# A two-layer hybrid encoder trunk on one core: own slots for two turned tiles, gates in two steps, memory rows later, last two quads by token tile

## Chip, cores and metric

The kernel runs on 1 core of one Trainium2 chip. The metric is device microseconds of one execution; the time given for a kernel is the median of its runs. Before the change it is 2223.97 us (3 runs, 2223.84 to 2224.96).

## What is computed

Input x (256 tokens x 2048 features, float32), a memory of 256 rows of the same width, and the weights of two layers. Each layer:

```
h    = rms_norm(x, norm_mix)
proj = h @ w_in          # g_q g_k 512 each, g_v g_r 1024 each, two gate ranks of 16, d_q d_k d_v m_q 512 each
mix  = concat( GLA(g_q, g_k, g_v, g_r, gates forward and backward),     # 4 heads, chunked, decays by log-sigmoid gates
               dilated window attention(d_q, d_k, d_v, relative bias),  # 4 heads
               attention of m_q to rms_norm(mem) @ w_mem_kv )           # 4 heads
x    = x + mix @ w_out
x    = x + square(relu(rms_norm(x) @ w_up)) @ w_down                    # 8192 wide
```

and one rms_norm at the end. All in float32.

## The kernel before

**Products.** Every large product goes through `linear` (L192): 256 tokens are two token tiles `t` of 128, the columns come 512 at a time into one PSUM bank per token tile, and the contraction in quads of 4 x 128 rows. A quad's weights (1 MB) are loaded by SP into one of three `raw` buffers (`load_quad`), ScalarE casts them to float32r (`wh`, L203), VectorE subtracts to get the low part (`wl`, L204), and TensorE makes three matmuls for each of 8 (row block, token tile) pairs: low x high, high x low, high x high (L221 to L223). `wh` and `wl` hold two quads. In the last quad of a product the matmuls are sorted by token tile.

**Left operands.** A left operand must lie transposed and split in the same way. x^T and mem^T of the first layer come transposed from the host (`split_loaded`). Everything else is turned on VectorE in 32x32 blocks, 16 instructions for a tile (`turn_blocks`, L108), then split (`parts_of`). `split_turned` and `heads_turned` are generators: `paced` makes the number of blocks that `steps` names and yields, and `turn(1)` advances the foremost one by a step. One `turn(1)` and one `flush(1)` (of `pending`, a queue of small jobs: squares of rows, loads) are called in each quad, behind that quad's last subtraction on VectorE. `turning` is first in, first out.

**Who sets the order.** The framework's planner orders the instructions of each engine by the order in which they are traced, by a timeline that it simulates, and by free buffers. A tile that finds no free slot waits, and what writes it is put later. Most tiles of 4 KB a partition share one ring of 22 slots (`slot`): turned and split operands, attention weights, gate tiles, `u` of the MLP. `work` has small pools: `junk` (2 buffers, target of squares whose sum alone is wanted), `E` (2 buffers of 6 KB), `dg` (2). `issue_after(i)` holds instructions of i's engine behind i.

**Start.** SP loads mem^T and the first three weight quads of the memory keys in turns, then `rel`, `onehot`, the memory rows (L497, four loads into x's buffer, for the sums of squares) and `ident`. The rest of the memory keys, the memory values (`ps_v`, in the auxiliary PSUM pool), column 9 of w_in (memory queries) and column 0 follow. When a chunk of memory rows has been squared, POOL loads the same chunk of x over it (L539). x^T is loaded by `plan_loads`, one step for each quad of the memory values.

**Mixing stage.** Column 1 (keys of GLA), memory attention (`attend_weights`, `attend_out`), `log_gates` (low-rank products, then exponential, logarithm, and a split into `gh`, `gl`), columns 2 and 3 (values of GLA), `gla_weights` (cumulative gates by matmuls with `tri`, exponentials into `E`, products with the turned queries and keys gqT and gkT), column 6 (dilated queries), and so on; then w_out, and the MLP in four parts of four groups of w_up and four of w_down.

**End.** After the last product each token tile adds its last chunk to x, sums squares, makes the reciprocal root on POOL (`rstd`) and scales four chunks on VectorE and ScalarE; SP stores them in two halves (L661 to L677).

Of the kernel before, what the change touches and what calls it, by code (L numbers as in the profile page):

```python
# [20 lines left out]
P = 128  # L21
# [21 lines left out]
def trunk_kernel(ctx: ExitStack, tc: tile.TileContext, a: dict):  # L43
# [12 lines left out]

    def turned_slot(name):
        return ring.tile([P, 4, S], F32, tag="o", name=name, bufs=2)
# [25 lines left out]
    class RowNorm:  # L84
# [6 lines left out]
        def add(self, c, t, v):  # L91
            junk = work.tile([P, NW], F32, tag="junk", name="junk")
            nc.scalar.activation(junk, v, AF.Square, accum_out=self.ssc[:, t, c:c + 1])  # L93
# [18 lines left out]
    def paced(turns, steps):  # L112
        for n in steps:
            for _ in range(n):
                next(turns)
            yield
# [75 lines left out]
    def linear(wsrc, lhs, quads, loaded=(), pool=ps_mm, tag="mm"):  # L192

        ps = [pool.tile([P, NW], F32, tag=tag, name=f"mm{t}") for t in range(NT)]
        nq = len(quads)
        for i, q in enumerate(quads):
            raw, n = loaded[i] if i < len(loaded) else load_quad(wsrc, q)
            wh = [wpool.tile([P, 2, NW], F32R, tag="wh", name="wh", bufs=4) for _ in range(2)]
            wl = [wpool.tile([P, 2, NW], F32R, tag="wl", name="wl", bufs=4) for _ in range(2)]
            n = min(4 // n, 2)  # L200
            for k in range(0, 4, n):
                hi, lo = (w[k // 2][:, k % 2:k % 2 + n] for w in (wh, wl))
                nc.scalar.activation(hi, raw[:, k:k + n], AF.Copy)  # L203
# [8 lines left out]
            xh, xl = lhs[q]  # L212
# [3 lines left out]
            for kk, t in order:  # L216
                sl = slice(t * P, (t + 1) * P)
                first = i == 0 and kk == 0
                last = i == nq - 1 and kk == 3
                hi, lo = wh[kk // 2][:, kk % 2, :], wl[kk // 2][:, kk % 2, :]  # L220
                nc.tensor.matmul(ps[t], xl[:, kk, sl], hi, start=first, stop=False)  # L221
                nc.tensor.matmul(ps[t], xh[:, kk, sl], lo, start=False, stop=False)  # L222
                nc.tensor.matmul(ps[t], xh[:, kk, sl], hi, start=False, stop=last)  # L223
            with tc.issue_after(cut.ins):
                flush(1)
        return ps
# [19 lines left out]
    tri = const.tile([P, 4, 2 * P], F32R, name="tri")  # L246
# [4 lines left out]
    onehot = work.tile([P, NW], F32, tag="junk", name="onehot")[:BUCKETS + 1]  # L251
# [12 lines left out]
    def late_constants():  # L264
        tri32 = work.tile([P, 4, 2 * P], F32, tag="E", name="tri32")
# [47 lines left out]
    def attend_out(weights, v, name):  # L313
# [5 lines left out]
        for t in range(NT):  # L319
            ps = aux([H, P], "pv")  # L320
            for h in range(H):
                for s in range(NT):
                    nc.tensor.matmul(  # L323
                        ps[:, h, :], pT[s][:, h, t * P:(t + 1) * P],
                        v[:, s, h * P:(h + 1) * P], start=s == 0, stop=s == NT - 1,
                    )
            ss = small.tile([P, H], F32, tag="ssh", name="ssh")
            for h in range(H):
                junk = work.tile([P, NW], F32, tag="junk", name="junk")
# [12 lines left out]

    def log_gates(lhs, rs, l):

        raw = slot([KT, 2 * RANK], "lrw")
# [5 lines left out]
        up32 = slot([2, NW], "up32")[:4 * RANK]  # L351
# [5 lines left out]
        gbias = slot([2, NW], "gbias")  # L357
# [12 lines left out]
        for d in range(2):  # L370
# [24 lines left out]
    def gla_weights(qT, kT, gates):  # L395
# [3 lines left out]
        for d in range(2):  # L399
            cr = slot([2, H, P], f"cr{d}")  # L400
            for i in range(NT):

                E = work.tile([P, 3, H, P], F32, tag="E", name="E")
                for h in range(H):
                    ps = aux([2 * P], "cum")
                    lo = slice(h * P, (h + 1) * P)
                    rhs = tri[:, 2 * d + i, :]
                    nc.tensor.matmul(ps, gl[d][:, i, lo], rhs, start=True, stop=False)
                    nc.tensor.matmul(ps, gh[d][:, i, lo], rhs, start=False, stop=True)
                    nc.scalar.activation(  # L410
                        E[:, 1:, h, :], ps.rearrange("p (b c) -> p b c", b=2), AF.Exp
                    )
                    nc.scalar.activation(E[:, 0, h, :], ps[:, :P], AF.Exp, scale=-1.0)
                tok = slice(i * P, (i + 1) * P)
                nc.vector.tensor_tensor(E[:, 0], kT[:, :, tok], E[:, 0], ALU.mult)
                nc.vector.tensor_tensor(E[:, 1], qT[:, :, tok], E[:, 1], ALU.mult)
# [3 lines left out]
                    cr[:, 0 if isk else 1], (kT if isk else qT)[:, :, tok], E[:, 2], ALU.mult  # L420
                )
                ps = aux([H, P], "dg")
                for h in range(H):
                    nc.tensor.matmul(ps[:, h, :], E[:, 0, h, :], E[:, 1, h, :], start=True, stop=True)  # L424

                dst = AT[i][:, i] if d == 0 else work.tile([P, H, P], F32, tag="dg", name="dg")
# [14 lines left out]
    def gla_out(AT, v):  # L441
        out = [slot([NT, NW], f"gla{c}") for c in range(2)]
        for c in range(2):
            for t in range(NT):
# [8 lines left out]
                for j in range(2):  # L453
                    junk = work.tile([P, NW], F32, tag="junk", name="junk")
# [45 lines left out]
    def plan_loads(name, loads, src, gain, lhs):  # L500


        def step(i):
            for q in loads[i] if i < len(loads) else ():
# [11 lines left out]
    for l in range(DEPTH):  # L516
# [4 lines left out]
        def keys_turned():  # L521
            turning.append(split_turned(km, "km", None, f"kmT{l}", heads, (0, 4, 4, 4, 4)))
# [6 lines left out]
        if l == 0:  # L529
            flush()  # L530
            bias_products()
            plan_loads("x0", ((0, 1), (2,), (3,)), a["xT"], gains[:, 0, 0, :], xlhs)
# [45 lines left out]
        mgain = gains[:, 1, l, :]  # L578
        turning.append(split_turned(o_mem, 3, mgain, "mT3", mlhs, (0, 4, 4, 4, 4)))
        gv = [evac(col(2 + c), rs, f"gv{c}") for c in range(2)]  # L580
# [39 lines left out]
        for part in range(FP):  # L620
            ulhs = {}
            for g in range(up_groups):
# [3 lines left out]
                u = slot([NT, NW], "u")  # L626
# [16 lines left out]
            for g in range(4):  # L643
# [4 lines left out]
                ps = linear(a["w_down"][l, part, g], ulhs, range(up_groups))  # L648
# [12 lines left out]
    for t in range(NT):  # L661
        v = xchunk(3, t)
        fnorm.add(3, t, v)
        rs = fnorm.done(t)
        for half in (1, 0):
            for c in (2 * half, 2 * half + 1):
                v = xchunk(c, t)
                if c == 3:
                    nc.vector.scalar_tensor_tensor(
                        v, v, rs[:, 0:1], fg[1][:, 1, :], ALU.mult, ALU.mult  # L670
                    )
                elif c == 1:
                    nc.vector.tensor_scalar(v, v, rs[:, 0:1], None, ALU.mult)
                else:
                    nc.scalar.activation(v, v, AF.Copy, scale=rs[:, 0:1])
            cs = slice(2 * half * NW, (2 * half + 2) * NW)
            nc.sync.dma_start(out_rows[:, t, cs], x[:, t, cs])  # L677
# [14 lines left out]
def _constants():  # L692
# [6 lines left out]
    for d, (inc, exc) in enumerate(((le, gt), (ge, lt))):  # L699
# [4 lines left out]
        for i in range(NT):  # L704
            isk = (i == 0) == (d == 0)
            sets.append(np.concatenate([middle, exc if isk else inc], 1))
# [70 lines left out]
```

## Time and profile before

| what | value |
|---|---|
| median of 3 runs | 2223.97 us |
| profiled execution | 2225.28 us, its span 2223.5 us |
| mean granted clock of TensorE | 0.994 |
| TensorE / VectorE / ScalarE busy | 98% / 71% / 51% |
| moved by DMA | 423.13 MB, mean 190 GB/s over the span |

The span runs from the first to the last instruction; the rest of an execution's time lies around it. In the rows PE is TensorE's matmuls, PEld its weight loads, DVE VectorE, ACT ScalarE, POOL GpSimd, SP the engine that issues most loads (SPq: the issuing instruction). A granted clock of 1.00 is 2.4 GHz, 0.50 is 1.2 GHz. A matmul's duration in the trace overlaps the next one's; the spacing of starts is what it takes.

### The profile page before, as it was taken

To read this page: it belongs to the slowest core of one execution; us is meant where nothing else is said; L and a number is where in the kernel's file an instruction comes from. 1 tells how busy PE (TensorE), PEld (TensorE's weight loads), DVE (VectorE), ACT (ScalarE), POOL (GpSimd) and SP (SyncE) were. 2 spreads that over 40 slices of the span, in tenths; PEclk is the share of its full clock that TensorE was granted. 3 is DMA by queue.
4 is the path that set the end of the run, shared out by engine and by line. 5 is a ranking of instruction groups with operands and counts; after the bars stand their busy time and mean duration, and the time that the engine had idled before them with its cause. 6 is when DMAs were issued, how large, how long until landed. Compare 5 with 4: busy or idle time off the path is not lost.

```text
span 2223.5 us, 25583 instructions
## 1 busy us (share of the span) xinstructions
PE 2184.5 (98%) x9834; PEld 1811.1 (81%) x9834; DVE 1588.5 (71%) x2210; ACT 1131.2 (51%) x1497; POOL 40.1 (2%) x69
## 2 busy tenths in 40 slices
PE   7998999999999999999999999999999999999998
PEld 5886888888888888888888887888888888888886
DVE  5658788886477577468977588788755764864774
ACT  7555565554354455345554554655544544543543
POOL 1000000000000000000000000000000000000000
PEclk9999999999999999999999999999999999999999
DMA  9643345555555555556555443455555555555553
GB/s 361 224 171 133 133 171 189 197 191 199 189 192 199 196 189 192 194 191 218 210 190 199 160 163 125 168 193 190 205 189 189 201 197 189 190 193 200 193 209 133
DMA packets 63362, 423.13 MB, mean 190 GB/s; under 512 B 7075, under 2 KB 7843, under 8 KB 14472
## 3 DMA queue, kind: packets, MB, share of 16 engines
q1 hardware_dynamic: 62104, 417.56, 53.8%
q0 software_dynamic: 1136, 3.94, 0.5%
q8 instruction: 77, 1.26, 0.2%
q14 instruction: 45, 0.37, 0.1%
HBM read 419.37 MB, written 3.15 MB: 190 GB/s over the span
## 4 chain that ended last, share of the span: by engine, by line
PE 94%; DVE 2%; DMA 2%; ACT 1%; issue 1%; SPq 0%; POOL 0%; ACTq 0%; POOLq 0%; DVEq 0%
PE mm L222 30%; PE mm L223 30%; PE mm L221 30%; DMA raw<-in_w_mem 1%; PE pv L323 1%; PE go L448 1%; DVE gkT L108 1%; DVE wl L204 0%; PE dg L424 0%; PE pT L309 0%; DVE gqT L108 0%; DMA x<-in_mem 0%; DVE dkT0o L108 0%; ACT junk L93 0%; ACT wh L203 0%
## 5 line engine op out<-in xcount | busy, mean ns | idle before, releaser
L204 DVE TENSOR_TENSOR wl<-raw,wh 128x1024 fp32r<-128x1024 f32 (+1 forms) x774 | 928.4, 1215 | 533.8 <-ACT wh L203 529.3
L203 ACT ACTIVATE wh<-raw 128x1024 fp32r<-128x1024 f32 (+1 forms) x774 | 813.9, 1053 | 887.2 <-PE mm L223 823.9
L222 PE MATMUL mm<-wl,uT2h 128*128 128x512 f32 x256 | 99.6, 389 | 0.0
L222 PE MATMUL mm<-wl,uT3h 128*128 128x512 f32 x256 | 99.6, 389 | 0.0
L223 PE MATMUL mm<-wh,uT3h 128*128 128x512 f32 x256 | 99.6, 389 | 0.0
L223 PE MATMUL mm<-wh,uT2h 128*128 128x512 f32 x256 | 99.6, 389 | 0.0
L221 PE MATMUL mm<-wh,zT0l 128*128 128x512 f32 x256 | 99.6, 389 | 0.0
L222 PE MATMUL mm<-wl,zT0h 128*128 128x512 f32 x256 | 99.6, 389 | 0.0
L223 PE MATMUL mm<-wh,zT0h 128*128 128x512 f32 x256 | 99.6, 389 | 0.0
L222 PE MATMUL mm<-wl,zT1h 128*128 128x512 f32 x256 | 99.6, 389 | 0.0
L223 PE MATMUL mm<-wh,zT1h 128*128 128x512 f32 x256 | 99.6, 389 | 0.0
L222 PE MATMUL mm<-wl,zT2h 128*128 128x512 f32 x256 | 99.6, 389 | 0.0
L223 PE MATMUL mm<-wh,zT2h 128*128 128x512 f32 x256 | 99.6, 389 | 0.0
L222 PE MATMUL mm<-wl,zT3h 128*128 128x512 f32 x256 | 99.6, 389 | 0.0
L223 PE MATMUL mm<-wh,zT3h 128*128 128x512 f32 x256 | 99.6, 389 | 0.0
L222 PE MATMUL mm<-wl,uT0h 128*128 128x512 f32 x256 | 99.6, 389 | 0.0
L223 PE MATMUL mm<-wh,uT0h 128*128 128x512 f32 x256 | 99.6, 389 | 0.0
L222 PE MATMUL mm<-wl,uT1h 128*128 128x512 f32 x256 | 99.6, 389 | 0.0
L223 PE MATMUL mm<-wh,uT1h 128*128 128x512 f32 x256 | 99.6, 389 | 0.0
L221 PE MATMUL mm<-wh,zT1l 128*128 128x512 f32 x256 | 99.4, 389 | 0.0
L221 PE MATMUL mm<-wh,uT1l 128*128 128x512 f32 x256 | 99.4, 389 | 0.0
L221 PE MATMUL mm<-wh,uT3l 128*128 128x512 f32 x256 | 99.3, 389 | 0.0
(428 smaller groups left out, 4637.5 us busy)
## 6 DMA issues: line engine op xcount, KB each, us to landing
raw<-in_w_up SPq DMA_DIRECT2D x128, 1024.0 KB, 4.8
raw<-in_w_down SPq DMA_DIRECT2D x128, 1024.0 KB, 4.8
raw<-in_w_in SPq DMA_DIRECT2D x80, 1024.0 KB, 4.8
raw<-in_w_out SPq DMA_DIRECT2D x32, 1024.0 KB, 4.8
raw<-in_w_mem SPq DMA_DIRECT2D x13, 1024.0 KB, 4.9
mem<-in_memT SPq DMA_DIRECT2D x7, 512.0 KB, 6.6
raw<-in_w_mem SPq DMA_DIRECT2D x12, 256.0 KB, 6.0
x<-in_mem SPq DMA_DIRECT2D x4, 512.0 KB, 6.8
```

Of the source, the lines that this page charges most:

```text
L108: yield nc.vector.transpose(dst[f:f + 32, :, :, s:s + 32], src[s:s + 32, :, :, f:f + 32])
L203: nc.scalar.activation(hi, raw[:, k:k + n], AF.Copy)
L204: cut = nc.vector.tensor_tensor(lo, raw[:, k:k + n], hi.bitcast(F32), ALU.subtract)
L221: nc.tensor.matmul(ps[t], xl[:, kk, sl], hi, start=first, stop=False)
L222: nc.tensor.matmul(ps[t], xh[:, kk, sl], lo, start=False, stop=False)
L223: nc.tensor.matmul(ps[t], xh[:, kk, sl], hi, start=False, stop=last)
L323: nc.tensor.matmul(ps[:, h, :], pT[s][:, h, t * P:(t + 1) * P], v[:, s, h * P:(h + 1) * P], start=s == 0, stop=s == NT - 1,)
L448: nc.tensor.matmul(ps[:, j, :], AT[s][:, t, 2 * c + j, :], v[c][:, s, j * DV:(j + 1) * DV], start=s == 0, stop=s == NT - 1,)
```

## The change

1. A second tag of two 4 KB slots in the ring's pool (`side_slot`) holds gqT, gkT and, in the MLP, `u`. `junk` and `dg` have one buffer each; `tri` holds three blocks of 128 columns for each direction in place of two pairs; the loads of `log_gates` go to `E` buffers.
2. `log_gates` ends with z and its clipped copy; exponential, logarithm and split are a function of their own, `gate_parts`, called after column 2's evacuation.
3. In layer 0 gk is evacuated before memory attention and both gq and gk are turned 8 blocks a step; in layer 1 memory attention stands before column 1. `paced` does not yield after its last step. Steps of km change.
4. What `turn` and `flush` issue on ScalarE in a quad is also held behind that quad's last cast.
5. The memory rows are loaded by the first four steps of x^T's plan, a chunk a step.
6. In the very last product the last two quads are ordered by token tile together, and the tail takes the sum of the first three chunks' squares ahead, skips one reduction, and stores in three pieces on two queues.

```diff
+    def side_slot(shape, name):
+        return ring.tile([P] + shape, F32, tag="t", name=name, bufs=2)
...
     def paced(turns, steps):
-        for n in steps:
+        for i, n in enumerate(steps):
             for _ in range(n):
                 next(turns)
-            yield
+            if i + 1 < len(steps):
+                yield
...
-    def heads_turned(v, name, heads):
+    def heads_turned(v, name, heads, steps):
-        o = slot([H, S], name)
-        yield from paced(turn_blocks(o, v), (0, 4, 4, 4, 4))
+        o = side_slot([H, S], name)
+        yield from paced(turn_blocks(o, v), steps)
...
-            with tc.issue_after(cut.ins):
+            with tc.issue_after(cut.ins), tc.issue_after(cast.ins):
                 turn(1)
...
-            order = [(kk, t) for kk in range(4) for t in range(NT)]
+            order += [(i, q, wh, wl, kk, t) for kk in range(4) for t in range(NT)]
+            if nq - late <= i < nq - 1:
+                continue
             if i == nq - 1:
-                order.sort(key=lambda o: o[1])
+                order.sort(key=lambda o: o[5])
...
+                    if late > 1 and t and done[0] is not None:
+                        queued.enter_context(tc.issue_after(done[0].ins))
...
-    tri = const.tile([P, 4, 2 * P], F32R, name="tri")
+    tri = const.tile([P, 2, 3 * P], F32R, name="tri")
...
-        raw = slot([KT, 2 * RANK], "lrw")
+        loaded = work.tile([P, 3, NW], F32, tag="E", name="lrup")
+        raw = loaded[:, 0].rearrange("p (k r) -> p k r", k=KT)
...
             nc.vector.scalar_tensor_tensor(ab[d], z[d], -1.0, z[d], ALU.mult, ALU.min)
+        return z, ab
+
+    def gate_parts(z, ab):
         for d in range(2):
             done = nc.scalar.activation(ab[d], ab[d], AF.Exp)
...
     with tc.issue_after(newest[0]):
-        for c in range(4):
+        nc.sync.dma_start(ident, a["ident"])
+
+    def load_rows(c):
+        with tc.issue_after(newest[0]):
             nc.sync.dma_start(x[:, :, c * NW:(c + 1) * NW], tokens(a["mem"], c))
-        nc.sync.dma_start(ident, a["ident"])
...
         def step(i):
+            if also is not None and i < 4:
+                also(i)
...
-            turning.append(split_turned(km, "km", None, f"kmT{l}", heads, (0, 4, 4, 4, 4)))
+            turning.append(split_turned(km, "km", None, f"kmT{l}", heads, (0, 6, 5, 5)))
...
-        turning.append(heads_turned(gq, "gqT", heads))
-        ps_gk = col(1)
-        while "mq" not in heads:
-            turn(1)
-        o_mem = attend_out(attend_weights(heads["mq"], heads["km"], None, "mem"), vm, "memo")
-        gk = evac(ps_gk, rs, "gk")
-        gates = log_gates(xlhs, rs, l)
-        turning.append(heads_turned(gk, "gkT", heads))
+        turning.append(heads_turned(gq, "gqT", heads, (0, 8, 8) if l == 0 else (0, 4, 4, 4, 4)))
+        if l == 0:
+            gk = evac(col(1), rs, "gk")
+            turning.append(heads_turned(gk, "gkT", heads, (0, 8, 8)))
+            o_mem = memory_attention()
+            gates = log_gates(xlhs, rs, l)
+        else:
+            o_mem = memory_attention()
+            gk = evac(col(1), rs, "gk")
+            gates = log_gates(xlhs, rs, l)
+            turning.append(heads_turned(gk, "gkT", heads, (0, 4, 4, 4, 4)))
         turning.append(split_turned(o_mem, 3, mgain, "mT3", mlhs, (0, 4, 4, 4, 4)))
-        gv = [evac(col(2 + c), rs, f"gv{c}") for c in range(2)]
+        gv = [evac(col(2), rs, "gv0")]
+        gates = gate_parts(*gates)
+        gv.append(evac(col(3), rs, "gv1"))
...
+                ending = end and last and g == 3
+                ps = linear(a["w_down"][l, part, g], ulhs, range(up_groups), late=2 if ending else 1)
+                if ending:
+                    continue
...
+        part = small.tile([P, 1], F32, tag="part", name="part")
+        nc.vector.tensor_reduce(part, fnorm.ssc[:, t, :3], AX.X, ALU.add)
+        nc.gpsimd.tensor_scalar(part, part, 1.0 / D, EPS, ALU.mult, ALU.add)
+        nc.vector.tensor_tensor(v, ps[t], v, ALU.add)
         fnorm.add(3, t, v)
-        rs = fnorm.done(t)
...
+        nc.gpsimd.tensor_scalar(m, fnorm.ssc[:, t, 3:], 1.0 / D, part[:, 0:1], ALU.mult, ALU.add)
...
+        nc.gpsimd.tensor_tensor(rs, m, neghalf[:, :1], ALU.pow)
...
+        nc.sync.dma_start(out_rows[:, t, :2 * NW], v[:, :2 * NW])
...
+        nc.sync.dma_start(out_rows[:, t, 3 * NW:], v[:, 3 * NW:])
...
+        nc.scalar.dma_start(out_rows[:, t, 2 * NW:3 * NW], v[:, 2 * NW:3 * NW])
```

## Rows read from the trace of the kernel before

**Rows 1.** The page, part 1: engine, busy us (share of the span), instructions.
```profile
PE 2184.5 (98%) x9834; PEld 1811.1 (81%) x9834; DVE 1588.5 (71%) x2210; ACT 1131.2 (51%) x1497; POOL 40.1 (2%) x69
```

**Rows 2.** Waits of TensorE: who waited <- for whom: us in total, times, longest.
```profile
PE mm L222 <- DVE wl L204: 18.4, 7, 9.9
PE mm L221 <- ACT wh L203: 10.4, 4, 5.1
```

**Rows 3.** Windows: length, busy us per engine, granted clock, DMA share, GB/s.
```profile
26.70:64.30 37.60, 30.32 (x122) 23.36 (x122) 20.82 (x31) 25.18 (x49) 5.59 (x10) 0.95 0.96 369
190.00:207.00 17.00, 7.14 (x25) 5.47 (x24) 16.56 (x33) 4.67 (x12) 0.00 (x0) 0.70 0.20 73
280.00:290.00 10.00, 8.50 (x38) 6.71 (x37) 9.90 (x15) 6.52 (x9) 0.00 (x0) 1.00 0.58 206
290.00:1290.00 1000.00, 1000.00 (x4504) 830.31 (x4502) 726.42 (x1008) 512.51 (x639) 11.65 (x14) 1.00 0.55 192
1290.00:1300.00 10.00, 7.94 (x28) 6.04 (x27) 9.83 (x16) 4.23 (x11) 0.00 (x0) 0.83 0.54 206
1370.00:1385.00 15.00, 12.04 (x48) 9.56 (x47) 14.75 (x26) 7.83 (x9) 0.00 (x0) 0.89 0.44 157
```

**Rows 4.** Timeline of TensorE, 200 to 207 us: start, us, what, [idle before <-releaser].
```profile
202.51 0.79 PE L222 MATMUL mm<-wl,x00h 128*128 128x512 f32 x1 [9.86 <-DVE wl L204]
...
205.66 0.39 PE L221 MATMUL mm<-wh,x00l 128*128 128x512 f32 x1
```

**Rows 5.** Timeline of TensorE, its last matmul.
```profile
2213.61 0.39 PE L223 MATMUL mm<-wh,uT3h 128*128 128x512 f32 x1
```

**Rows 6.** Timeline of VectorE, 186 to 205 us.
```profile
186.22 7.17 DVE L108 STREAM_TRANSPOSE gqT<-gq 32x256 f32<-32x256 f32 x16
193.42 7.18 DVE L108 STREAM_TRANSPOSE gkT<-gk 32x256 f32<-32x256 f32 x16
...
201.24 3.49 DVE L204 TENSOR_TENSOR wl<-raw,wh 128x1024 fp32r<-128x1024 f32 x3
```

**Rows 7.** The tile gqT: ns min/median/max, first and last start.
```profile
L108 DVE STREAM_TRANSPOSE gqT<-gq x32: 425/436/442, 186.2 to 1226.9; 32x256 f32<-32x256 f32 x32
```

**Rows 8.** Timeline of VectorE in layer 1, 1285 to 1376 us.
```profile
1285.09 7.18 DVE L108 STREAM_TRANSPOSE gkT<-gk 32x256 f32<-32x256 f32 x16
...
1370.77 2.69 DVE L108 STREAM_TRANSPOSE dkT1o<-dk 32x256 f32<-32x256 f32 x6
```

**Rows 9.** Timeline of TensorE, 1366 to 1384 us.
```profile
1376.38 0.79 PE L222 MATMUL mm<-wl,xT0h 128*128 128x512 f32 x1 [2.96 <-DVE wl L204]
```

**Rows 10.** Timeline of VectorE in an MLP group, 455 to 464 us.
```profile
457.63 2.36 DVE L204 TENSOR_TENSOR wl<-raw,wh 128x1024 fp32r<-128x1024 f32 x2
459.91 1.29 DVE L122 TENSOR_TENSOR uT0l<-uT0o,uT0h 128x512 fp32r<-128x512 f32 x2
```

**Rows 11.** Timeline of TensorE in the same group.
```profile
461.32 0.61 PE L221 MATMUL mm<-wh,zT3l 128*128 128x512 f32 x2
```

**Rows 12.** Timeline of SP (DMA issues), 13 to 36 us.
```profile
15.18 2.39 SPq L497 DMA_DIRECT2D x<-in_mem  x4
...
19.55 0.82 SPq L189 DMA_DIRECT2D raw<-in_w_mem  x2
```

**Rows 13.** DMA from 10 to 60 us; issues: xcount, KB each, us to landing.
```profile
DMA packets 5532, 19.27 MB, mean 385 GB/s; under 512 B 650, under 2 KB 778, under 8 KB 4575
...
raw<-in_w_mem SPq DMA_DIRECT2D x5, 1024.0 KB, 15.2
```

**Rows 14.** Timeline of TensorE, 26 to 31 us.
```profile
29.09 0.73 PE L221 MATMUL mm<-wh,mem03l 128*128 128x512 f32 x2 [2.39 <-ACT wh L203]
```

**Rows 15.** Timeline of VectorE, 2211 to 2224 us.
```profile
2214.57 0.48 DVE L673 TENSOR_SCALAR x<-x,r_fin 128x512 f32<-128x512 f32 x1
2214.96 0.68 DVE L471 TENSOR_TENSOR x<-mm,x 128x512 f32<-128x512 f32 x1
2216.49 0.16 DVE L99 TENSOR_REDUCE ss_fin<-ssc_fin 128x1 f32<-128x4 f32 x1 [0.85 <-ACT junk L93]
```

More of the change, by code (lines that the diff above doesn't have):

```diff
@@ L91, in add @@
         def add(self, c, t, v):
-            junk = work.tile([P, NW], F32, tag="junk", name="junk")
+            junk = work.tile([P, NW], F32, tag="junk", name="junk", bufs=1)
             nc.scalar.activation(junk, v, AF.Square, accum_out=self.ssc[:, t, c:c + 1])
@@ L190, in load_quad, with linear @@
         return raw, pieces
-    def linear(wsrc, lhs, quads, loaded=(), pool=ps_mm, tag="mm"):
+    def linear(wsrc, lhs, quads, loaded=(), pool=ps_mm, tag="mm", late=1):
         ps = [pool.tile([P, NW], F32, tag=tag, name=f"mm{t}") for t in range(NT)]
-        nq = len(quads)
+        nq, order, done = len(quads), [], [None] * NT
         for i, q in enumerate(quads):
@@ L202, in linear @@
                 hi, lo = (w[k // 2][:, k % 2:k % 2 + n] for w in (wh, wl))
-                nc.scalar.activation(hi, raw[:, k:k + n], AF.Copy)
+                cast = nc.scalar.activation(hi, raw[:, k:k + n], AF.Copy)
                 cut = nc.vector.tensor_tensor(lo, raw[:, k:k + n], hi.bitcast(F32), ALU.subtract)
-            with tc.issue_after(cut.ins):
+            with tc.issue_after(cut.ins), tc.issue_after(cast.ins):
                 turn(1)
@@ L211, in linear @@
                     turn(1)
-            xh, xl = lhs[q]
-            order = [(kk, t) for kk in range(4) for t in range(NT)]
+            order += [(i, q, wh, wl, kk, t) for kk in range(4) for t in range(NT)]
+            if nq - late <= i < nq - 1:
+                continue
             if i == nq - 1:
-                order.sort(key=lambda o: o[1])
-            for kk, t in order:
+                order.sort(key=lambda o: o[5])
+            for j, p, wh, wl, kk, t in order:
+                xh, xl = lhs[p]
                 sl = slice(t * P, (t + 1) * P)
-                first = i == 0 and kk == 0
-                last = i == nq - 1 and kk == 3
+                first = j == 0 and kk == 0
+                last = j == nq - 1 and kk == 3
                 hi, lo = wh[kk // 2][:, kk % 2, :], wl[kk // 2][:, kk % 2, :]
[L221 to L224, printed above, removed]
+                with ExitStack() as queued:
+                    if late > 1 and t and done[0] is not None:
+                        queued.enter_context(tc.issue_after(done[0].ins))
+                    nc.tensor.matmul(ps[t], xl[:, kk, sl], hi, start=first, stop=False)
+                    nc.tensor.matmul(ps[t], xh[:, kk, sl], lo, start=False, stop=False)
+                    m = nc.tensor.matmul(ps[t], xh[:, kk, sl], hi, start=False, stop=last)
+                if last:
+                    done[t] = m
+            order = []
+            with tc.issue_after(cut.ins), tc.issue_after(cast.ins):
                 flush(1)
@@ L250, in trunk_kernel @@
     rel = work.tile([BUCKETS + 1, H], F32, name="rel", bufs=1)
-    onehot = work.tile([P, NW], F32, tag="junk", name="onehot")[:BUCKETS + 1]
+    onehot = work.tile([P, NW], F32, tag="junk", name="onehot", bufs=1)[:BUCKETS + 1]
     rows = work.tile([P, NW], F32, tag="E", name="rows")[:H]
@@ L264, in late_constants @@
     def late_constants():
-        tri32 = work.tile([P, 4, 2 * P], F32, tag="E", name="tri32")
+        tri32 = work.tile([P, 2, 3 * P], F32, tag="E", name="tri32")
         nc.sync.dma_start(tri32, a["tri"])
@@ L328, in attend_out @@
             for h in range(H):
-                junk = work.tile([P, NW], F32, tag="junk", name="junk")
+                junk = work.tile([P, NW], F32, tag="junk", name="junk", bufs=1)
                 nc.scalar.activation(
@@ L350, in log_gates @@
         nc.vector.tensor_tensor(split[:, :, 1], raw, split[:, :, 0].bitcast(F32), ALU.subtract)
-        up32 = slot([2, NW], "up32")[:4 * RANK]
+        up32 = loaded[:4 * RANK, 1:]
         nc.sync.dma_start(up32, a["up"][l])
@@ L356, in log_gates @@
         nc.vector.tensor_tensor(upl, up32, uph.bitcast(F32), ALU.subtract)
-        gbias = slot([2, NW], "gbias")
+        gbias = work.tile([P, 3, NW], F32, tag="E", name="gbias")[:, :2]
         nc.sync.dma_start(gbias, a["gbias"][l].partition_broadcast(P))
@@ L406, in gla_weights @@
                     lo = slice(h * P, (h + 1) * P)
-                    rhs = tri[:, 2 * d + i, :]
+                    rhs = tri[:, d, i * P:(i + 2) * P]
                     nc.tensor.matmul(ps, gl[d][:, i, lo], rhs, start=True, stop=False)
                     nc.tensor.matmul(ps, gh[d][:, i, lo], rhs, start=False, stop=True)
+                    middle = slice((1 - i) * P, (2 - i) * P)
                     nc.scalar.activation(
@@ L423, in gla_weights @@
                 for h in range(H):
-                    nc.tensor.matmul(ps[:, h, :], E[:, 0, h, :], E[:, 1, h, :], start=True, stop=True)
-                dst = AT[i][:, i] if d == 0 else work.tile([P, H, P], F32, tag="dg", name="dg")
+                    nc.tensor.matmul(ps[:, h, :], E[:, 0, h, :], E[:, 2 - i, h, :], start=True, stop=True)
+                dst = AT[i][:, i] if d == 0 else work.tile([P, H, P], F32, tag="dg", name="dg", bufs=1)
                 nc.gpsimd.memset(dst, 0.0)
@@ L453, in gla_out @@
                 for j in range(2):
-                    junk = work.tile([P, NW], F32, tag="junk", name="junk")
+                    junk = work.tile([P, NW], F32, tag="junk", name="junk", bufs=1)
                     nc.scalar.activation(
@@ L495, in trunk_kernel, with plan_loads @@
     with tc.issue_after(newest[0]):
-        for c in range(4):
+        nc.sync.dma_start(ident, a["ident"])
+    def load_rows(c):
+        with tc.issue_after(newest[0]):
             nc.sync.dma_start(x[:, :, c * NW:(c + 1) * NW], tokens(a["mem"], c))
-        nc.sync.dma_start(ident, a["ident"])
-    def plan_loads(name, loads, src, gain, lhs):
+    def plan_loads(name, loads, src, gain, lhs, also=None):
         def step(i):
+            if also is not None and i < 4:
+                also(i)
             for q in loads[i] if i < len(loads) else ():
@@ L531, in trunk_kernel @@
             bias_products()
-            plan_loads("x0", ((0, 1), (2,), (3,)), a["xT"], gains[:, 0, 0, :], xlhs)
+            plan_loads("x0", ((0, 1), (2,), (3,)), a["xT"], gains[:, 0, 0, :], xlhs, load_rows)
             ps_v = linear(a["w_mem"][l, 1], mem_lhs, range(4), pool=ps_ax, tag="ax")
@@ L568, in trunk_kernel, with memory_attention @@
             gq = evac(col(0), rsq, "gq")
[L569 to L576 removed]
         mlhs = {}
         mgain = gains[:, 1, l, :]
+        def memory_attention():
+            while "mq" not in heads:
+                turn(1)
+            return attend_out(attend_weights(heads["mq"], heads["km"], None, "mem"), vm, "memo")
+        turning.append(heads_turned(gq, "gqT", heads, (0, 8, 8) if l == 0 else (0, 4, 4, 4, 4)))
[9 more added lines that the diff above has]
+            turning.append(heads_turned(gk, "gkT", heads, (0, 4, 4, 4, 4)))
         turning.append(split_turned(o_mem, 3, mgain, "mT3", mlhs, (0, 4, 4, 4, 4)))
[L580 removed]
+        gv = [evac(col(2), rs, "gv0")]
+        gates = gate_parts(*gates)
+        gv.append(evac(col(3), rs, "gv1"))
         while "gkT" not in heads:
@@ L625, in trunk_kernel @@
                     rs = znorm.done()
-                u = slot([NT, NW], "u")
+                u = side_slot([NT, NW], "u")
                 for t in range(NT):
@@ L662, in trunk_kernel @@
         v = xchunk(3, t)
+        part = small.tile([P, 1], F32, tag="part", name="part")
+        nc.vector.tensor_reduce(part, fnorm.ssc[:, t, :3], AX.X, ALU.add)
+        nc.gpsimd.tensor_scalar(part, part, 1.0 / D, EPS, ALU.mult, ALU.add)
+        nc.vector.tensor_tensor(v, ps[t], v, ALU.add)
         fnorm.add(3, t, v)
-        rs = fnorm.done(t)
[L665 to L677, printed above, removed]
+        m = small.tile([P, 1], F32, tag="m1", name="m_fin")
+        nc.gpsimd.tensor_scalar(m, fnorm.ssc[:, t, 3:], 1.0 / D, part[:, 0:1], ALU.mult, ALU.add)
+        rs = small.tile([P, 1], F32, tag="rs_fin", name="r_fin")
+        nc.gpsimd.tensor_tensor(rs, m, neghalf[:, :1], ALU.pow)
+        v = x[:, t, :]
+        nc.scalar.activation(v[:, :NW], v[:, :NW], AF.Copy, scale=rs[:, 0:1])
+        nc.vector.tensor_scalar(v[:, NW:2 * NW], v[:, NW:2 * NW], rs[:, 0:1], None, ALU.mult)
+        nc.sync.dma_start(out_rows[:, t, :2 * NW], v[:, :2 * NW])
+        nc.vector.scalar_tensor_tensor(
+            v[:, 3 * NW:], v[:, 3 * NW:], rs[:, 0:1], fg[1][:, 1, :], ALU.mult, ALU.mult
+        )
+        nc.sync.dma_start(out_rows[:, t, 3 * NW:], v[:, 3 * NW:])
+        nc.scalar.activation(v[:, 2 * NW:3 * NW], v[:, 2 * NW:3 * NW], AF.Copy, scale=rs[:, 0:1])
+        nc.scalar.dma_start(out_rows[:, t, 2 * NW:3 * NW], v[:, 2 * NW:3 * NW])
 def _bucket(rel):
@@ L703, in _constants @@
         middle = plus.astype(np.float32) - minus
-        for i in range(NT):
-            isk = (i == 0) == (d == 0)
-            sets.append(np.concatenate([middle, exc if isk else inc], 1))
+        sets.append(np.concatenate([inc if d else exc, middle, exc if d else inc], 1))
     tri = np.stack(sets, 1).astype(np.float32) / 16.0
```

7 lines of the change are left out of this document (3 added, 4 removed).

## Prediction

> **What bounds the kernel now.** I read the page first: TensorE is busy for 98% of the span [rows 1]. So only its idle time, its time at the lower clock, and what lies after its last matmul can be won. Next the waits of TensorE: nearly all its idle time is waiting for a weight quad to be split, 18.4 us for VectorE's low part and 10.4 us for ScalarE's high part [rows 2]. Then the windows say where: in the long MLP stretch from 290 to 1290 us TensorE is busy without a break at full clock; the losses are in five short places [rows 3]. Idle is a window's length less its PE column, and (1 - granted clock) x length is about what the lower level took from it:
> - 26.7 to 64.3 us (memory projections): 37.60 - 30.32 = 7.28 us idle, and 0.05 x 37.6 = 1.9 us of clock.
> - 190 to 207 us (layer 0, first quad after the gates): 9.86 us idle in one wait, then the half clock: eight rows from 202.51 to 205.66 us are 7 intervals of 0.45 us, where a quad of 24 matmuls in 5.44 us at full clock gives 0.227: 1.56 us [rows 4].
> - 280 to 290 us: 1.50 us idle.
> - 1290 to 1300 us (layer 1, the place of the 9.86 us): 2.06 + 0.17 x 10 = 3.8 us.
> - 1370 to 1385 us: 2.96 + 0.11 x 15 = 4.6 us.
>
> Together 9.2 us at the start and 11.4 + 1.5 + 3.8 + 4.6 = 21.3 us in the two mixing stages. The last matmul ends at 2214.00 us [rows 5], and a tail of 9.5 us follows.
>
> **The change part by part.**
>
> *Own slots for gqT and gkT, gates in two steps.* The 9.86 us wait is a queue on VectorE. The low parts of the quad that TensorE wants start at 201.24 us; ahead of them stand 16 transposes of gq and 16 of gk, 7.17 + 7.18 = 14.35 us without a gap, from 186.22 us [rows 6]. In layer 1 gq's last transpose starts at 1226.9 us [rows 7], long before the gates, and only gk's 7.18 us pile up at 1285.09 us [rows 8]; there the wait is 2.06 us. The transposes came this late, I read, because their target had no free ring slot until the gate tiles were done. With two slots of their own (later lent to u, whose turn is over within one group of quads), and with the exponentials and logarithms put behind gv0, the 14.35 us can go into columns 1 to 3 of w_in. The lower bound of what this takes away is 0 (the planner may still put them late), the upper 11.4 + 3.8 = 15.2 us. I take all of 15.2: the work is unchanged, and VectorE, 16.56 of 17.00 us busy in this place, has 27 us in every 100 free in the MLP stretch, where TensorE never waits [rows 3]. If the cover is gone, one batch of 7.2 us costs what layer 1 shows, 3.8 us.
>
> *Memory attention before or after gk, paced steps.* Same instructions in another order. What is late next is the turn of dk: its last eight transposes, from 1370.77 us, and a subtraction among them [rows 8] hold the quad whose low parts TensorE lacks for 2.96 us until 1376.38 us [rows 9]. The turns are first in, first out, so with gq, gk and the memory output gone sooner, dq and dk come sooner. But nothing pulls them apart, and they still share columns with the GLA products. Bounds 0 and 1.5 + 4.6 = 6.1 us; I take the middle, 3.
>
> *Parts in the same step as the last blocks.* `paced` no longer stops after its last step, so the two halves of a turned tile are cut in the third quad, not the fourth: 1.29 us of VectorE move ahead of the next quad's cut, in all 32 groups of w_up. In the trace the first of that quad's two cuts ends at about 457.63 + 1.2 = 458.9 us [rows 10], and TensorE begins the quad at 461.32 us [rows 11]: 2.4 us of cover over 1.29. I take 0; the end without cover is a rival below. The new order of ScalarE's copies behind the quad's cast delays only what VectorE cuts next, and ScalarE is 51% busy [rows 1].
>
> *Smaller edits.* `junk` with one buffer: after the one-hot table, which TensorE reads before the first square, all writers are ScalarE's, in order; 0. `dg` with one buffer: the second memset waits for an addition with a token tile's GLA work in between; 0. `tri` as three blocks: the same matmuls and exponentials on other columns; 0. Gate loads in the E slots: SP finds their slots free a column earlier; 0, and if a slot is late, the raw loads queued behind on SP are too (three buffers, so some two quads, 10 us, of cover). For all of them together the bounds are a loss of 2 us and a gain of 1.
>
> *Memory rows loaded later.* Before, four loads of 512 KB go out on SP at 15.18 us, and the fourth weight quad is issued behind them at 19.55 us [rows 12]. Around it the DMA engines move 385 GB/s on average [rows 13], so these 2.1 MB cost that quad 2.1 / 0.385 = 5.4 us. TensorE waited 2.39 us for it [rows 14]: gone. Now the rows travel one 512 KB piece behind each quad of the second projection. Each of those needs 1 MB of weights, 0.5 MB of rows and about 0.5 MB of x^T in 5.44 us, which is 385 GB/s: just what there is. So of the other 4.9 us idle and 1.9 us of clock I take two thirds: 2.4 + 4.6 = 7 us. Bounds 0 and 9.2. Queued behind the rows on SP are x^T and the next raw quad; the squares of memory on ScalarE, and behind them the four loads of x on POOL, come later, but they are wanted only for evacuations a column (over 20 us) on.
>
> A rule of the Trainium skill speaks against this part ("DMA: Bandwidth & Descriptors", section "Issuing engines are not separate DMA queues"): transfers issued from SP and from POOL end on the same 16 engines and interleave. The trace agrees: with x coming in over POOL at the same time, a weight quad takes 15.2 us to land here [rows 13]. By that rule alone the sum for this part would be 0.
>
> *Last two quads by token tile, new tail.* Before, token tile 0 is done 12 matmuls (2.72 us) before the end; now 24 (5.44 us). Its scaling on VectorE, still running at 2214.57 + 0.48 us, then no longer stands between the last matmul and tile 1's addition, which began at 2214.96 us [rows 15] and can now begin at 2214.06: 0.9 us. The reduction of 0.16 us and its handover leave the chain: 0.25 us [rows 15]. The last store is split in three on two queues; 1 MB still has to move, so I take 0.2. Sum 1.35 us, bounds 0 and 2.5. The strict order needs the last quad's low parts 2.72 us sooner; two quads of slots hold them.
>
> **Sum.** 15.2 + 3 + 7 + 1.35 = 26.5 us. The profiled execution took 2225.28 us (a span of 2223.5 us and 1.8 around it), so 2198.8 us. The median of the runs shown is 1.31 us under the profiled one: the forecast is 2197.5 us.
>
> **Rivals.**
> - *All five places close.* 9.2 + 21.3 + 2 = 32.5 us: 2191.5. For it: queues and their order explain all five. Against: dk is only helped indirectly.
> - *The start is bound by its bytes.* The total up to 64 us is unchanged, and moving 2.1 MB within it gains nothing: 26.5 - 7 = 19.5 us, 2204.5. Against: the fourth quad's wait is one of order, and x, not weights, can be the late one. The section of the Trainium skill named above would have it come out this way.
> - *The slots were not the cause (the change doesn't do what it says).* The planner still groups gq and gk late, or the gates meet them behind gv0; layer 0 keeps its 11.4 us and layer 1 its 3.8: 26.5 - 15.2 = 11.3 us, 2212.7. For it: rows 6 show the order, not its reason.
> - *Slower: the third quad overflows.* ScalarE's copy of the parts waits for both casts (2 x 1.06 us), VectorE stands for it in order and then cuts (1.29), and the next quad's cut comes after: 0.6 + 2.1 + 1.3 = 4.0 us against 2.4 us of cover. From 2.4 us on TensorE waits; here 1.6 us in each of 32 groups, 51 us: 2249. For it: 0.73 of VectorE's time is taken there already [rows 3]. Against: the cut is ready first and need not stand behind.
>
> **How the numbers follow.** Forecast 0.47, all closed 0.14, bytes 0.17, slots 0.14, overflow 0.08. Within 0.2% (4.4 us), about the least that a measurement of this kernel can tell from no change, lie only mixtures in which a new wait eats most of a gain; I give them 0.09, out of the faster cases. So faster 0.83, same 0.09, slower 0.08. The range goes from 2190 (a little beyond all closed) to 2213 (the slot rival) and leaves out the overflow and the mixtures.
>
> **What would show it.** Right: no wait of TensorE over 1 us at the first quad after the gates in either layer; gqT and gkT transposed before gh and gl; the fourth memory quad without a wait; tile 1's addition within 0.2 us of the last matmul; 290 to 1290 us as full as before. Wrong: gqT and gkT still in blocks of 7 us ahead of a cut; the same 7 us idle between 26 and 60 us; waits of TensorE of one size in every MLP group, or the lower clock in a place where it was full.

## The result, and the profile after

The changed kernel takes 2195.45 us (median of 4 runs, 2195.25 to 2195.68) against 2224.47 us before (4 runs, 2223.84 to 2225.69): ratio 0.9869, 95% interval 0.9852 to 0.9886, 29.0 us less. The forecast was 2197.5 us, 26.5 us less. The span fell from 2223.5 to 2193.9 us.

The page of the changed kernel, part 1 (answers to [rows 1]), then all its waits of TensorE (to [rows 2]):

```profile
PE 2176.4 (99%) x9834; PEld 1807.1 (82%) x9834; DVE 1587.2 (72%) x2210; ACT 1134.8 (52%) x1497; POOL 42.8 (2%) x71
```

```profile
PE mm L231 <- ACT wh L208: 5.5, 1, 5.5
PE sc L249 <- ACT dkT0h L125: 1.2, 1, 1.2
PE sc L249 <- ACT dkT1h L125: 1.2, 1, 1.2
PE mm L231 <- DVE mem01l L132: 0.9, 1, 0.9
PE mm L232 <- DVE wl L209: 0.4, 2, 0.2
```

VectorE and ScalarE are as busy as before; only idle time of TensorE went. The first row is the wait for the very first quad, which was there before (5.1 us). Of the five places two small ones are left, at the scores of the dilated branch, where dk is turned too late, once in each layer. In the windows (length, busy per engine, granted clock, DMA) the memory projections are full at 410 GB/s, the stretch after the gates in layer 0 is full with VectorE at 19.71 of 20.00 us, and the MLP stretch is as it was [rows 3]:

```profile
26.70:54.10 27.40, 27.40 (x123) 22.69 (x122) 18.51 (x27) 16.51 (x26) 2.97 (x5) 1.00 1.02 410
170.00:190.00 20.00, 20.00 (x95) 16.78 (x94) 19.71 (x27) 13.90 (x21) 0.00 (x0) 1.00 0.48 160
290.00:1290.00 1000.00, 1000.00 (x4496) 830.18 (x4495) 729.06 (x1009) 509.83 (x631) 11.35 (x14) 1.00 0.56 191
```

The tiles gqT and gkT, first and last start over both layers (answers to [rows 7], where gqT began at 186.2 us):

```profile
L111 DVE STREAM_TRANSPOSE gqT<-gq x32: 425/436/441, 116.6 to 1213.8; 32x256 f32<-32x256 f32 x32
L111 DVE STREAM_TRANSPOSE gkT<-gk x32: 425/436/441, 136.5 to 1249.7; 32x256 f32<-32x256 f32 x32
```

To place the gains I read four marks off TensorE's timeline of every run: the first matmul of column 9, the first of w_up in layer 0, the first of column 9 in layer 1, and the end of the last. They cut a span into start, layer 0's mixing with w_out, the MLP with the memory projections, everything to the last matmul, and the tail (us; runs described below):

```
                       start   layer 0     MLP  layer 1 on   tail     span
before                 64.29    358.95  739.88     1050.88   9.51   2223.5
after                  54.08    347.52  739.92     1044.03   8.35   2193.9
e1_ring_slots          53.60    358.43  739.87     1042.01   8.58   2202.5
e2_gates_at_once       55.63    347.52  739.90     1041.98   8.35   2193.4
e3_rows_early          56.98    347.52  739.92     1044.04   8.34   2196.8
e4_rows_early_pool     58.14    347.51  739.86     1044.00   8.65   2198.2
e5_yield_back          54.00    352.15  739.91     1048.73   8.57   2203.4
e6_cast_order_off      53.47    348.47  739.88     1044.04   8.48   2194.3
e8_loads_in_ring       55.75    347.35  739.87     1044.03   9.32   2196.3
e9_layer1_order_old    53.75    347.51  739.87     1043.81   8.35   2193.3
b1_own_slots_alone     62.04    358.38  739.90     1045.88   9.95   2216.1
b2_rows_late_alone     53.76    359.12  739.86     1050.83   9.42   2213.0
b3_cast_order_alone    58.74    359.71  739.84     1050.40   9.41   2218.1
n1_dk_side             53.75    345.79  739.87     1042.03   8.34   2189.8
```

So the change gave 10.2 us at the start, 11.4 in layer 0, 6.9 from layer 1 on and 1.2 in the tail. The MLP column does not move by 0.1 us in any run. Each row is one execution, and the start scatters: e2 and e8, whose edits leave it alone, have 55.6 and 55.8 us. In e2 TensorE waits 1.8 us for a part of mem^T (0.9 in the changed kernel), and the granted clock is 0.89 from 10 to 25 us. So a difference of 2 us in that column alone says little.

### The profile page after: what moved, and what is told of

The parts are those of the page before. It is cut to its first block, busy times and chain, and to the rows that moved or that the text cites. A ratio compares the mean times of both kernels' runs of the same rounds, so it can differ in the third digit from the quotient of the medians.

```text
span 2193.9 us, 25587 instructions
## 1 busy us (share of the span) xinstructions
PE 2176.4 (99%) x9834; PEld 1807.1 (82%) x9834; DVE 1587.2 (72%) x2210; ACT 1134.8 (52%) x1497; POOL 42.8 (2%) x71
## 3 DMA queue, kind: packets, MB, share of 16 engines
q1 hardware_dynamic: 62104, 416.90, 55.6%
## 4 chain that ended last, share of the span: by engine, by line
PE 98%; DVE 1%; DMA 0%; ACT 0%; SPq 0%; issue 0%; POOL 0%; POOLq 0%; ACTq 0%
PE mm L232 31%; PE mm L233 31%; PE mm L231 31%; PE pv L336 1%; PE go L466 1%; PE dg L442 0%; PE pT L322 0%; DMA raw<-in_w_mem 0%; DVE dkT0o L111 0%; DVE dkT1o L111 0%; PE sc L251 0%; PE sc L250 0%; PE cum L426 0%; PE cum L425 0%; PE lrps L377 0%
```

## Experiments

Names with e undo a part of the changed kernel, b do one part alone on the kernel before, n goes further. Each has at least four runs.

**Own slots undone (e1).**
```diff
-        return ring.tile([P] + shape, F32, tag="t", name=name, bufs=2)
+        return ring.tile([P] + shape, F32, tag="r", name=name)
```


> The changed kernel with gqT, gkT and u back in the ring of 22 slots; all else stays. If the slots are the cause of the two waits after the gates (9.9 and 2.1 us before), both or at least layer 0's come back with their half clock: 2195.5 + 11 to 15 = 2206 to 2211 us, gqT and gkT transposed in one run of 14 us ahead of a cut. If the gates in two steps and the new order do it, the time stays at 2195 to 2198 us.

Measured 2204.5 us (2204.26 to 2206.19). Layer 0 lost 10.9 us, layer 1 on gained 2.0. VectorE's timeline before the wait, and TensorE's row with it:

```profile
162.99 7.18 DVE L111 STREAM_TRANSPOSE gqT<-gq 32x256 f32<-32x256 f32 x16
170.19 3.57 DVE L111 STREAM_TRANSPOSE gkT<-gk 32x256 f32<-32x256 f32 x8
173.79 2.36 DVE L405 SCALAR_TENSOR_TENSOR z<-z,ab 128x1024 f32<-128x1024 f32 x2
176.19 3.60 DVE L111 STREAM_TRANSPOSE gkT<-gk 32x256 f32<-32x256 f32 x8
179.81 1.23 DVE L209 TENSOR_TENSOR wl<-raw,wh 128x1024 fp32r<-128x1024 f32 x1
```

```profile
181.09 0.80 PE L232 MATMUL mm<-wl,x02h 128*128 128x512 f32 x1 [8.83 <-DVE wl L209]
```

The same queue as in [rows 6], some two quads earlier. In layer 0 the change needs the slots; in layer 1 other edits close the waits without them.

**Own slots alone (b1)**, with what makes room for them in SBUF (one `junk` and one `dg` buffer, `tri` in three blocks).
```diff
-        o = slot([H, S], name)
+        o = side_slot([H, S], name)
...
-                u = slot([NT, NW], "u")
+                u = side_slot([NT, NW], "u")
```


> The kernel before the change with own slots for gqT, gkT and u, and with what makes room for them (one junk and one dg buffer, tri in three blocks). With the ring back (e1) layer 0 lost 8.8 us again and layer 1 nothing. If the slots alone close layer 0's wait and its half clock, 11.4 us go: 2212 to 2214 us, gqT and gkT turned before the gates. If they also close layer 1's two places, 2205 to 2208 us. If they need the new order, 2222 to 2225 us.

Measured 2219.59 us (10 runs, 2217.44 to 2221.02). The turns do come early, but layer 0 gains only 0.6 us; layer 1 on gains 5.0. In layer 0 TensorE now waits for PSUM: gv of both value columns is evacuated in one go, behind the gates. And at dk it waits 3.2 us, where 1.5 us were idle before. That is 8.7 us of idle time in layer 0 in place of 11.4, with a lower clock behind both waits; before, only the first had one [rows 3]. gqT in this kernel, ScalarE's timeline, TensorE's row, the wait at dk and its window:

```profile
L111 DVE STREAM_TRANSPOSE gqT<-gq x32: 425/436/442, 129.8 to 1224.1; 32x256 f32<-32x256 f32 x32
```

```profile
185.09 2.00 ACT L388 ACTIVATE ab<-ab 128x1024 f32<-128x1024 f32 x2
187.00 1.99 ACT L206 ACTIVATE wh<-raw 128x1024 fp32r<-128x1024 f32 x2
188.90 1.99 ACT L394 ACTIVATE gh<-z 128x1024 fp32r<-128x1024 f32 x2
190.79 2.40 ACT L234 ACTIVATE gv<-mm,r_mix 128x512 f32<-128x512 f32 x4
```

```profile
191.51 0.80 PE L224 MATMUL mm<-wh,x00l 128*128 128x512 f32 x1 [5.29 <-ACT gv L234]
```

```profile
PE sc L239 <- ACT dkT0h L124: 3.2, 1, 3.2
```

```profile
270.00:290.00 20.00, 16.61 (x66) 13.16 (x66) 19.62 (x35) 10.02 (x12) 0.00 (x0) 0.91 0.48 158
```

So the slots are necessary in layer 0 and not enough. gv stood behind the gates in the kernel before too, evacuated from 185.0 us on; TensorE did not wait for it there. Here it comes at 190.8 us. Whether gv lacks a slot here, so that the shortage passes on to it, or only follows the gates because it is traced behind them, no run separates. None of the three expected cases came.

b1's start is 2.3 us shorter, before any side slot is used. With one `junk` buffer the first square of the memory rows waits on ScalarE until TensorE has read the one-hot table; it starts at 23.81 us, not 21.11:

```profile
23.81 0.63 ACT L96 ACTIVATE junk<-x 128x512 f32<-128x512 f32 x1 [3.14 <-PE biasps L259]
```

The casts of the fourth quad stand behind the squares on ScalarE, and TensorE's wait for that quad grows from 2.4 to 4.5 us. Of the 4.4 us of later waits, up to 52 us, 1.2 are left.

**Gates in one step again (e2).**
```diff
-        return z, ab
+        return gate_parts(z, ab)
...
-        gates = gate_parts(*gates)
```


> The changed kernel with gate_parts called at the end of log_gates, as before the change. By the slot theory the turns are out of the way already and TensorE waits at most 1 us more in each layer: 2195.5 to 2197.5 us. If it is the two-step gates that free VectorE, layer 0's wait comes back: 2203 to 2210 us.

Measured 2193.45 us (2192.98 to 2195.42): layer 0 the same, layer 1 on 2.0 us shorter than in the changed kernel, which neither expected case had. Beside the other edits the two steps buy nothing, and in layer 1 they are a little in the way: dk's evacuations there run to 1328.4 us, to 1337.1 in the changed kernel, and the wait at its scores is gone.

**Gate loads back in the ring, and the old order of the last quads (e8).** Two places that the trace keeps apart.
```diff
-        loaded = work.tile([P, 3, NW], F32, tag="E", name="lrup")
-        raw = loaded[:, 0].rearrange("p (k r) -> p k r", k=KT)
+        raw = slot([KT, 2 * RANK], "lrw")
...
-    ... late=2 if ending else 1)
+    ... late=1)
```


> The changed kernel with two edits undone in two places that the trace keeps apart: the three loads of log_gates back in ring slots, and only the last quad sorted by token tile at the end. End: tile 1's addition again 0.9 us late, so the time from the last matmul to the end of the span 0.5 to 0.9 us longer. Layer 1: if it is the ring's three freed slots that closed its two waits (2.1 and 3.0 us before), they come back, 3 to 8 us in all: 2199 to 2204 us together. If another order closed them, 2196 to 2196.5 us.

Measured 2196.21 us (2195.75 to 2198.1). Both layers stay as they are, so these three slots are not needed beside the rest. The tail is 0.97 us longer. The last matmul began at 2186.62 us and ended at 2187.01; tile 1's addition, the last row, waited behind tile 0's scaling again (VectorE, L709 and L711):

```profile
2187.34 0.75 DVE L711 SCALAR_TENSOR_TENSOR x<-x,r_fin,fg 128x512 f32<-128x512 f32 x1
2188.00 0.68 DVE L701 TENSOR_TENSOR x<-mm,x 128x512 f32<-128x512 f32 x1
```

In the changed kernel TensorE's last matmul and that addition (answers to [rows 5, 15]) are 0.04 us apart:

```profile
2185.16 0.39 PE L233 MATMUL mm<-wh,uT3h 128*128 128x512 f32 x1
```

```profile
2185.59 0.69 DVE L702 TENSOR_TENSOR x<-mm,x 128x512 f32<-128x512 f32 x1 [1.67 <-PE mm L233]
```

**Layer 1's old order (e9).**
```diff
-            o_mem = memory_attention()
-            gk = evac(col(1), rs, "gk")
+            ps_gk = col(1)
+            o_mem = memory_attention()
+            gk = evac(ps_gk, rs, "gk")
```


> The changed kernel with column 1 ahead of memory attention again in layer 1, as before. If this order is what closed layer 1's two waits, 3.8 to 8 us come back after 1270 us: 2199 to 2204 us. If the slots did, no change: 2195 to 2196 us.

Measured 2194.99 us (2194.8 to 2195.44): no difference. The order in layer 1 is worth nothing here.

**A yield after the last step again (e5).**
```diff
-            if i + 1 < len(steps):
-                yield
+            yield
```


> The changed kernel with paced yielding after its last step again, so that parts are cut a quad later everywhere. The overflow rival (parts ahead of the third quad's successor cost time in all 32 groups of w_up) would make it faster by several us, with the MLP stretch shorter. The forecast's term says 0 there. In the mixing stages a quad more for each turn can bring dk later still: 2195 to 2199 us.

Measured 2204.82 us (2203.69 to 2206.68). Beyond both expected cases: not the MLP, but both mixing stages became longer, by 4.6 and 4.7 us. TensorE's waits at dk, and the window of the layer 0 one, with the clock that the wait cost:

```profile
PE sc L248 <- ACT dkT1h L124: 3.2, 1, 3.2
PE sc L248 <- ACT dkT0h L124: 3.2, 1, 3.2
```

```profile
255.00:275.00 20.00, 16.80 (x62) 13.17 (x61) 19.62 (x35) 9.22 (x12) 0.00 (x0) 0.83 0.32 106
```

The small edit in `paced` is what brings dk sooner: a turn ends one call earlier, and the queue behind it moves up. The wait of 3.2 us was followed by half clock (0.17 x 20 = 3.4 us lost), the one of 1.2 us in the changed kernel was not.

**Memory rows early again, on SP (e3) and on POOL (e4).** e3 restores the four loads ahead of `ident`; e4 issues them from POOL:
```diff
+    for c in range(4):
+        nc.gpsimd.dma_start(x[:, :, c * NW:(c + 1) * NW], tokens(a["mem"], c))
```


> The changed kernel with the four loads of memory rows back ahead of the fourth weight quad on SP. If late rows are what freed the start, column 9 begins at about 64 us, not 54, with 7 us of idle between 26 and 60 us: 2204 to 2206 us. If another edit did it (ScalarE's copies held behind the casts), at most 3 us come back: 2196 to 2198.5 us.

> The changed kernel with all memory rows early, but issued by POOL, so that no weight quad stands behind them on SP. If the fourth quad waited because of the order on SP's queue, the wait of 2.4 + 0.5 us stays away: 2195 to 2197 us. If the bytes decide, since both queues share the DMA engines, the wait is there as with rows early on SP, or larger as the rows now start with the first quads: 2199 to 2204 us.

Measured 2199.91 us (2198.78 to 2201.24) and 2199.88 us (2199.4 to 2201.33). In e3 only the fourth quad's wait of [rows 14] is back; in e4 it is not, but the first quad of all waits instead. TensorE's rows of e3, then of e4:

```profile
28.84 0.73 PE L231 MATMUL mm<-wh,mem03l 128*128 128x512 f32 x2 [2.36 <-ACT wh L208]
30.10 0.50 PE L232 MATMUL mm<-wl,mem03h 128*128 128x512 f32 x1 [0.53 <-DVE wl L209]
```

```profile
10.36 1.22 PE L231 MATMUL mm<-wh,mem00l 128*128 128x512 f32 x2 [1.70 <-ACT wh L208]
14.04 1.22 PE L231 MATMUL mm<-wh,mem00l 128*128 128x512 f32 x2 [0.75 <-ACT wh L208]
```

Column 9 begins 2.9 and 4.1 us later than in the changed kernel. On another queue the 2 MB cost as much, so the order on SP's queue alone does not decide; that they move ahead of the weights does. (In e4 they also start sooner, at 1.28 us against 14.95 in e3, and meet other quads. Rows on POOL at the time of e3 were not tried.) That the other 7 us stayed away with early rows asked for a second cause.

**One edit alone on the kernel before: the cast order (b3), the late rows (b2); and the cast order undone (e6).**
```diff
-            with tc.issue_after(cut.ins):
+            with tc.issue_after(cut.ins), tc.issue_after(cast.ins):
                 turn(1)
```
(and the same at `flush(1)`; b2 is the change's `load_rows`.)

> The kernel before the change with one edit: what turn and flush issue on ScalarE in a quad is held behind that quad's last cast. With the rows early again (e3) only 2.9 us of idle came back at the start, and the squares of the memory rows, which free x's buffer for x itself, ran at 58 us, not at 21 to 27. Theory: this edit, not the late rows, closes the waits at 41 to 52 us, because the 2 MB of x leave the stretch in which DMA is full: column 9 begins at 57 to 58 us, not 64.3, and the time is 2217 to 2219 us. Rival (rows, paced steps or the slots do it): no change at the start, 2223 to 2226 us.

> The kernel before the change with one edit: the memory rows one chunk a step in x^T's plan. If lateness of the rows is worth only the fourth quad's wait, column 9 begins 3 to 4 us sooner and the time is 2220 to 2222 us. If it was the whole of the start, as the prediction had it, 54 to 57 us and 2214 to 2218 us. If later squares meet the casts of the values, nothing or a loss: 2224 to 2230 us.

> The changed kernel without the holding of ScalarE's work behind the cast. If this holding closes most of the start, 4 to 7 us of idle and half clock come back between 40 and 60 us: 2199 to 2203 us. If late rows alone do, nothing: 2195 to 2196 us. The MLP stretch stays full in either case.

Measured: b3 2219.92 us (9 runs, 2218.11 to 2220.62), start 5.6 us shorter; b2 2215.61 us (2214.77 to 2216.19), start 10.5 us shorter; e6 2196.85 us (2196.11 to 2197.4), start unchanged, layer 0 longer by 0.9 us, which is between the two expected cases. Each edit suffices for the later waits. The loads of x on POOL show by which way; in the kernel before they went out from 22.88 to 27.11 us. First and last of four, in b2 and in b3:

```profile
29.36 0.78 POOL L543 DMA_DIRECT2D x<-in_x  x1 [3.37 <-ACT junk L93]
...
49.10 0.72 POOL L543 DMA_DIRECT2D x<-in_x  x1 [4.69 <-ACT junk L93]
```

```profile
61.52 0.73 POOL L539 DMA_DIRECT2D x<-in_x  x1 [16.82 <-ACT junk L93]
...
73.63 0.71 POOL L539 DMA_DIRECT2D x<-in_x  x1 [0.51 <-ACT junk L93]
```

b3 holds the squares of memory behind the casts, so x is loaded after the full stretch; b2 spreads rows and x over it, and still feeds every quad in time. At the start both together give no more than the late rows alone.

**One step further (n1): dk in a side slot.**
```diff
-        dk = evac(col(7), rs, "dk")
+        dk = evac(col(7), rs, "dk", side_slot)   # evac takes its tile from the function given
```


> The changed kernel with dk evacuated into one of the two side slots, free once gqT is used up. If dk comes 20 us after its column because of a missing ring slot, it is evacuated at about 230 us in layer 0, not 249, the waits of 1.4 us at the dilated scores go in both layers: 2192.5 to 2193.5 us. If it is the order of the turns, nothing moves: 2195 to 2196 us.

Measured 2191.38 us (2191.2 to 2191.7), 0.9848 of the kernel before (0.9833 to 0.9862); every run lies some 4 us under every run of the changed kernel. dk's evacuation in the changed kernel and in n1, and n1's waits of TensorE, which are only the first two quads':

```profile
L244 ACT ACTIVATE dk<-mm,r_mix x4: 687/690/694, 249.1 to 1337.1; 128x512 f32<-128x512 f32 x4
```

```profile
L244 ACT ACTIVATE dk<-mm,r_mix x4: 682/687/693, 228.5 to 1314.5; 128x512 f32<-128x512 f32 x4
```

```profile
PE mm L231 <- ACT wh L208: 5.2, 1, 5.2
PE mm L231 <- DVE mem01l L132: 1.7, 1, 1.7
```

dk was late for want of a ring slot, as gq had been. 3.7 of the 4.1 us of span come from the two layers; the rest is the start.

## Why the prediction was right, and where not

- *The sum.* 26.5 us were forecast, 29.0 measured; the difference is the start, 10.2 us for 7. The two mixing stages gave 18.3 us for 15.2 + 3 forecast, so near by some luck: the 3 was the middle of its bounds, and the edits share the 18.3 otherwise than the prediction had it.
- *Own slots and gates in two steps, 15.2 us taken.* Both waits after the gates are gone. Right as the cause of the 9.86 us wait (e1: 10.9 us in layer 0), wrong that slots and two steps do all of it: the two steps are not needed (e2), the slots alone give 0.6 us in layer 0 and 5.0 from layer 1 on (b1), because gv behind the gates and dk hold TensorE next, which the prediction did not look for; and with the other edits layer 1 does not need the slots (e1). Which edit brings gv in time in layer 0 is open: two steps (e2), gate loads (e8) and the yield (e5) were each taken away alone, and none brought that wait back. Two of them together, and the new order in layer 0, were not tried.
- *dk, 3 us taken of 6.1.* A turn that ends a call sooner does bring dk sooner, but by the missing yield, worth 4.6 and 4.7 us (e5); the prediction priced that edit at 0 for the MLP, which is right, and did not follow it into the mixing stages. And order was not all: dk also lacked a ring slot. Of the 6.1 us two waits of 1.2 us were left, worth 1.7 and 2.0 us, and n1 took them.
- *The rival of the third quad* is refuted: the MLP column is 739.9 us with and without the yield. VectorE cuts the next quad ahead of the parts, as it did before [rows 10]; in the changed kernel:

```profile
457.75 2.36 DVE L209 TENSOR_TENSOR wl<-raw,wh 128x1024 fp32r<-128x1024 f32 x2
460.03 1.29 DVE L126 TENSOR_TENSOR uT1l<-uT1o,uT1h 128x512 fp32r<-128x512 f32 x2
```

- *Rows late, 7 us taken, bounds 0 and 9.2.* It was 10.2 us, above the bound. The idle 7.28 us went, but TensorE's busy time in the stretch fell too, by 2.9 us (30.32 to 27.40), where the prediction had only 1.9 for the clock: a wait also costs at its edges, and there were six. The two matmuls behind one take 0.73 us [rows 14]; a pair at full pace in the changed kernel takes 0.62 us. b2 shows that the edit alone gives all of it. The stretch now moves 410 GB/s, more than the 385 that the prediction took for all there is. The order of ScalarE's copies, priced at 0, gives 5.6 us alone, and beside the late rows nothing at the start and 0.9 us in layer 0 (e6).
- *The start bound by its bytes* did not come. e4 moved the rows to another issuing engine and lost as much as e3, which agrees with the rule of the Trainium skill behind that rival ("DMA: Bandwidth & Descriptors", section "Issuing engines are not separate DMA queues"). The step from "the same engines" to "no gain" failed: the total need not be in before the weights.
- *Tail, 1.35 us.* Measured 1.16: 0.97 for the order of the last quads (e8, 0.9 predicted), 0.2 for the rest (0.45 predicted), no more than the tails scatter between runs that leave them alone (8.34 to 8.65 us).
- *Smaller edits, 0.* For `junk` the reason given is wrong: the first square does wait for TensorE's reading of the one-hot table, 3.14 us in b1. With the rows late this costs the changed kernel nothing that its waits show. The gate loads are worth 0 (e8); `dg` and `tri` were not taken alone.

## What to carry to other kernels

A tile that waits for a buffer shows as an instruction that comes late while its engine had been idle; look what freed the buffer, and expect another tile to hold the engine next when one gets a slot of its own. In a stretch where DMA is full, ask which bytes must be in by when, not how many there are. Undo every edit by itself: of this change some were worth 10 us, some nothing, and the gates in two steps lost 2.

## What was not expected of the hardware

Waits of the same length cost differently. Two waits of TensorE of 1.2 us left the granted clock at 1.00. The two waits of 3.2 us in e5 were each followed by 6.8 us at half clock (0.83 over 20 us), but the one of 3.2 us at the same place in b1 by about half of that (0.91 over 20 us). In the kernel before, 1.50 us cost no clock, and 2.06 and 2.96 us were followed by some 3.4 us at half clock each [rows 3].
